# Stick-breaking attention on one Trainium2 core: the first logits ten gate steps earlier, the softplus issued in written order, splits one step behind the sum

## The chip, the cores and the metric

The kernel runs on one core of a Trainium2 chip. The metric is the device time of one execution in microseconds (us). The kernel before takes 1889.11 us, the median of three runs.

The engines are named as in the profile: PE is the matmul engine (PEld its weight loads), DVE the vector engine, ACT the scalar engine, POOL GpSimd, SP the queue that issues the transfers.

## The reference

A decoder trunk of two layers on 512 tokens of width 2048, in float32. The first layer attends to the top keys picked by an indexer, the second is stick-breaking attention over shared keys and values. The change lies in the second:

```python
def mixer_b(x, w_in, w_o, k, v):
    q, gate = jnp.split(x @ w_in, [WIDTH_B], axis=-1)
    ...
        z = jnp.einsum('bqngd,bsnd->bngqs', qg, k).astype(jnp.float32) * (HEAD_DIM ** -0.5)
        strict = key_pos[None, :] < t[:, None]
        log_om = jnp.where(strict, -jax.nn.softplus(z), 0.0)
        suffix = lax.cumsum(log_om, axis=log_om.ndim - 1, reverse=True) - log_om
        a = jnp.where(strict, jnp.exp(jax.nn.log_sigmoid(z) + suffix), 0.0)
        o = jnp.einsum('bngqs,bsnd->bqngd', a.astype(v.dtype), v)
    ...
    return (o * jax.nn.silu(gate)) @ w_o
```

There are 16 query heads in 4 groups; each group shares one head of keys and values. Then come a layer norm and a gated embedding.

## The kernel before

**Split products.** Every float32 operand is split into a high part (ACT copies it to a reduced format, names ending in `h`) and a low part (DVE subtracts, names ending in `l`); `split` does both. `mm3` multiplies high by high, high by low and low by high: three matmuls of 128x512 into one PSUM bank. A *gate step* below is one `mm3` of the gate projection.

**Streams.** Weights arrive through `next_raw` in three buffers `raw`, issued on SP. `Ahead(items, 2)` splits them two items ahead into `wh` and `wl`, three buffers each. `gate_items` also reads back the second half of the eight activation blocks that the Strassen products had overwritten, from `x2` in DRAM, and queues their splits (`restore`, tiles `xh` and `xl`).

**Order.** PE runs in program order (`manual_schedule`). The other engines are ordered by the tile framework's scheduler, except instructions marked by `keep_in_program_order`, which keep their order among themselves. `Paced` marks whatever is issued while `pinned[0]` is set. `bg` is a queue of small pieces of work; `pumped` issues one of them behind each gate step, through `paced`, which pins it.

**The second layer.** Keys, values and queries are Strassen products (loop at L1088, the last one, n == 4, gives the queries of group 3). `combine` adds up the seven products M, first on ACT and DVE, then by three `onto` pieces. Then (L1101 to L1150) the first keys are split, the four query blocks of group 0 and the four value blocks, one piece behind each of the first nine gate steps; 20 gate steps of group 0 run before the pool of the work tiles `px` opens, in the place of the values' unsplit tile.

**Sticks.** `sticks(g, Q)` goes through ten units, the pairs (query block i, key block kb) with kb from i down to 0: unit 0 is (0,0), unit 1 (1,1), unit 2 (1,0), unit 3 (2,2) and so on. The units 0, 1, 3 and 6 are diagonal. For each unit:

- `logits(u)`: z on PE; softplus as Abs, Exp, Ln on ACT and a sum on DVE; the mask `strict` on POOL (L1157) on diagonal units; the split into `sh`, `sl`.
- `weights(u)`: matmuls of `tri` and `neg` by the split softplus add the suffix sums onto z (L1199); Exp on ACT; mask on diagonal units; split into `ah`, `al`.
- `values(u)`: product with the split values into the bank o.

In round s it runs logits(s), weights(s-1), values(s-2), with a yield behind each, and `interleave` puts gate steps of the same group between the yields: 40 of them over 34 yields in group 0 (20 were done before), 52 over 34 in groups 1 to 3, where 8 run ahead. Group 0 has four more yields ahead of its first weights, and so have the others. Behind each group its banks are gated by Silu, which needs another activation table than Exp and Ln; `preload_act_table_set` puts the log and exp table back at the head of each group.

Of the kernel before, what the change touches and what calls it, by code (L numbers as in the profile page):

```python
# [51 lines left out]
def steps(gen, n):  # L52
    for _ in range(n):
        next(gen, None)
# [23 lines left out]
def trunk_kernel(  # L78
# [50 lines left out]
    def split(hi, lo, src, eng=dve):  # L129
        act.activation(hi, src, AF.Copy)  # L130
        eng.tensor_tensor(lo, src, hi.bitcast(F32), ALU.subtract)
# [171 lines left out]
    bg = deque()  # L303

    def paced(fn, *args):
        pinned[0] = True
        fn(*args)
        pinned[0] = False

    def one():  # L310
        paced(bg.popleft())
# [1 line left out]
    def pumped(gen, every=1):  # L313

        for i, _ in enumerate(gen):
            if bg and i % every == 0:
                one()
            yield

    def drain():  # L320
        while bg:
            one()
# [59 lines left out]
    def quarter(x, i, j0=0, rows=2):  # L382

        j = j0 + rows * (i % 2 == 0)
        t = H * (i in (1, 2))
        return x[:, j : j + rows, t : t + H]

    def combine(wp, M, dst):

        m1, m2, m6, m7, m5, m3, m4 = M  # L390
        u = wp.tile([128, 2, H], F32, name="u", tag="u", bufs=1)[:, : m1.shape[1]]
        c11, c22, c12, c21 = (dst(i) for i in range(4))
        pinned[0] = True
        act.activation(u, m1, AF.Copy)
        act.activation(c21, m7, AF.Copy)
        act.activation(c12, m5, AF.Copy)
        dve.tensor_tensor(c11, m2, u, ALU.add)
        dve.tensor_tensor(u, m6, u, ALU.add)
        pinned[0] = False

        def onto(c):
            dve.tensor_tensor(c, c, u, ALU.add)

        def rest():
            dve.tensor_tensor(c22, c12, c21, ALU.add)
            dve.tensor_tensor(c12, m3, c12, ALU.add)
            dve.tensor_tensor(c21, c21, m4, ALU.subtract)

        paced(rest)
        return [lambda c=c: onto(c) for c in (c12, c21, c22)]  # L410
# [124 lines left out]
    def mm_banks(name):  # L535
        return [bank(j, name) for j in range(4)]
# [531 lines left out]
    finish_layer(0, xT, x2, (pk_, pv_), first_sums, first_blocks)  # L1068


    with ps_:
        sp = ps_.enter_context(tc.tile_pool(name="sp1", bufs=1))
        C3.extend(c3_tiles(sp, range(4, 8)))
        Kf, Vf = shared
        banks = [bank(b, "k") for b in range(4)]
        gemm = gemm_w(kitems, plain, banks, order=PAIRS)
        items = first_chunk(gemm, TF, T1, C3, lambda: strassen_stream([512] * 5, sp))
        for g in range(4):
            act.activation(Kf[:, g], banks[g], AF.Copy)

        def turn_values(t):
            s = slice(t * 128, (t + 1) * 128)
            ps = bank(2, "vt")
            for g in range(4):
                pe.transpose(ps[:, g * 128 : (g + 1) * 128], Vf[:, g, s], ident)
            act.activation(Vf[:, :, s], ps.rearrange("p (g d) -> p g d", g=4), AF.Copy)

        for n, dst in enumerate((Vf, *F)):  # L1088
            M = product_banks(4 - n)
            gemm = pumped(gemm_s(items, C3, M), 8)  # L1090
            if n == 1:
                steps(gemm, 40)
                for t in range(4):
                    steps(gemm, 16)
                    turn_values(t)
            run(gemm)
            drain()
            bg.extend(combine(sp, M, lambda i: quarter(dst, i)))
        drain()

# [5 lines left out]
    def split_keys(g):  # L1106
        K[g] = tuple(pc.tile([128, T], F32R, name=f"k{s}", tag=f"k{s}", bufs=2) for s in "hl")
        split(*K[g], Kf[:, g])

    def split_values(t):  # L1110
        split(*V[t], Vf[:, :, t * 128 : (t + 1) * 128])
# [5 lines left out]
        dve.scalar_tensor_tensor(ql, src, HSCALE, qh.bitcast(F32), ALU.mult, ALU.subtract)  # L1117
        Q[i] = tuple(a.rearrange("p h q -> p (h q)") for a in (qh, ql))

    def restore(raw, k):  # L1120
        split(XH[k][:, H:T], XL[k][:, H:T], raw[:, k % 4])

    def gate_items():
        for k, n in ((0, 6), (4, 2)):
            yield from plain_items([(512, n)])
            raw = next_raw()
            bg.extend(lambda raw=raw, k=k: restore(raw, k) for k in range(k, k + 4))
        yield from plain_items([(512, 8), *[(512, NK)] * 3])

    items = Ahead(gate_items(), 2)  # L1130

    def gate_first(banks):

        for kb in (*range(8, NK), *range(8)):
# [3 lines left out]
                mm3(out, (wh[:, s], wl[:, s]), plain(kb), kb == 8, kb == 7)  # L1138
                yield

    bg.append(lambda: split_keys(0))
    for i in range(4):
        bg.append(lambda i=i: split_scaled(0, i))
        bg.append(lambda i=i: split_values(i))
    banks = mm_banks("g")
    gemm = pumped(gate_first(banks))
    steps(gemm, 20)
    pv_.close()
    px_ = ExitStack()
    px = px_.enter_context(ss(name="px", bufs=1, side="right"))  # L1150

    def work():
        return px.tile([128, 512], F32, name="wk", tag="wk", bufs=4)
# [5 lines left out]
    def sticks(g, Q):  # L1159
        units = [(i, kb) for i in range(4) for kb in range(i, -1, -1)]  # L1160
        later = {}
        running = {}
        state = {}
        out = {}

        def logits(u):
            i, kb = units[u]
            z = spare("z")
            ks = slice(kb * 128, (kb + 1) * 128)
            mm3(z, [k[:, ks] for k in K[g]], Q[i], True, True)  # L1170
            e = work()
            keep = kb == i > 1
            sp = px.tile([128, 512], F32, name="run", tag="run", bufs=2) if keep else work()
            act.activation(e, z, AF.Abs)
            act.activation(e, e, AF.Exp, scale=-1.0)
            act.activation(e, e, AF.Ln, bias=1.0)
            dve.scalar_tensor_tensor(sp, z, 0.0, e, ALU.max, ALU.add)
            if kb == i:
                strict(sp)
            parts = tuple(px.tile([128, 512], F32R, name=f"s{s}", tag=f"s{s}", bufs=4) for s in "hl")  # L1180
            split(*parts, sp)
            state[u] = z, parts
            if keep:
                running[i] = sp
            if kb == i:
                later[u + 1] = parts
            elif kb:
                below = tuple(px.tile([128, 512], F32R, name=f"r{s}", tag=f"s{s}", bufs=4) for s in "hl")
                dve.tensor_tensor(running[i], running[i], sp, ALU.add)
                dve.tensor_copy(below[0], running[i])  # L1190
                dve.tensor_tensor(below[1], running[i], below[0].bitcast(F32), ALU.subtract)
                later[u + 1] = below

        def weights(u):
            i, kb = units[u]
            z, parts = state[u]
            terms = [(neg, p) for p in (later[u] if kb < i else ())] + [(tri, p) for p in parts]
            for n, (m, p) in enumerate(terms, 1):
                pe.matmul(z, m, p, start=False, stop=n == len(terms), skip_group_check=True)  # L1199
            a = work()  # L1200
            act.activation(a, z, AF.Exp)
            if kb == i:
                strict(a)
            parts = tuple(px.tile([128, 512], F32R, name=f"a{s}", tag=f"a{s}", bufs=2) for s in "hl")
            split(*parts, a)
            state[u] = parts

        def values(u):
            i, kb = units[u]
            if kb == i:  # L1210
                out[i] = bank(7, "o")
            mm3(out[i], [v[:, g] for v in V[kb]], state.pop(u), kb == i, kb == 0)
            if kb == 0:
                act.activation(F[g][:, :, i * 128 : (i + 1) * 128], out[i].rearrange("p (h q) -> p h q", h=4), AF.Copy)

        for s in range(12):
            for fn, u in ((logits, s), (weights, s - 1), (values, s - 2)):
                if s == 1 and fn == weights:
                    for _ in range(4):
                        yield  # L1220
                if 0 <= u < 10:
                    fn(u)
                    yield

    for g in range(4):
        tc.keep_in_program_order(act.preload_act_table_set("natural_log_exp_and_others"))
        if g:
            banks = mm_banks("g")
            gemm = pumped(gemm_w(items, plain, banks))
        if g < 3:  # L1230
            bg.append(lambda g=g: split_keys(g + 1))
        interleave(sticks(g, Q), 30 + 4, gemm, 52 if g else 40, lead=8 * (g > 0))
        if g < 3:
            for i in range(4):
                split_scaled(g + 1, i)
        for h in range(4):
            sg = work()
            act.activation(sg, banks[h], AF.Silu)
            dve.tensor_tensor(F[g][:, h], F[g][:, h], sg, ALU.mult)
# [52 lines left out]
```

## Time and profile before

| | |
|---|---|
| median of 3 runs | 1889.11 us (1888.52 to 1889.22) |
| the profiled execution | 1889.62 us |
| its span | 1887.9 us |
| PE busy | 1874.2 us (99%) |
| DVE, ACT, POOL busy | 1220.4, 928.5, 28.4 us |
| chain that ended last, by engine | PE 96%, DVE 2%, ACT 1%, DMA 1% |

The span runs from the first to the last instruction of the profiled execution. A timeline row gives start, duration, engine, line, operation, the tiles out<-in and their shapes; the bracket at its end is the idle time of the engine ahead of it and what ended it. The stick-breaking stage lies between about 1243 and 1513 us.

### The profile page before, as it was taken

Reading aid. Unit: us, or ns where it says so; the run is one execution under the profiler, and the core shown is the slowest. Engines: PE = TensorE matmul, PEld = TensorE weight load, DVE = VectorE, ACT = ScalarE, POOL = GpSimd, SP = SyncE. Lnnn points to the kernel's source line nnn. Section 1 sums busy time; section 2 is a strip of 40 time slices with the busy share of each in tenths; the row PEclk is TensorE's granted clock in tenths of the full one; section 3 lists DMA queues with packets and bytes.
Section 4 is the critical chain, followed back from the end, with each engine's and each line's share of the span. In section 5 each row is a group of like instructions: output and inputs, shape, how many; then the busy total and the mean of one; then the engine's idle time right before and its main releaser. Section 6 shows DMA issues by size and latency. Waiting matters only on the chain.

```text
span 1887.9 us, 25064 instructions
## 1 busy us (share of the span) xinstructions
PE 1874.2 (99%) x9229; PEld 1584.7 (84%) x9229; DVE 1220.4 (65%) x2385; ACT 928.5 (49%) x1692; POOL 28.4 (2%) x49
## 2 busy tenths in 40 slices
PE   9999999999999999999999999999999999999998
PEld 7898888888888888888888999987888888888887
DVE  5668879966556454675368788876655545567534
ACT  4446323355554432474245444468877743347422
POOL 0000000000000000000000000000100000000000
PEclk9999999999999999999999999999999999999999
DMA  5432333312222532333343333331122153242333
GB/s 185 137 114 65 101 90 100 101 56 68 67 68 60 165 110 78 124 100 106 117 134 113 106 97 111 101 112 57 56 68 68 57 189 98 75 129 89 123 101 112
DMA packets 110587, 189.22 MB, mean 100 GB/s; under 512 B 8240, under 2 KB 28208, under 8 KB 110464
## 3 DMA queue, kind: packets, MB, share of 16 engines
q1 hardware_dynamic: 110320, 187.33, 32.3%
q8 instruction: 72, 1.18, 0.3%
q14 instruction: 51, 0.42, 0.1%
q0 software_dynamic: 144, 0.30, 0.1%
HBM read 179.21 MB, written 8.39 MB: 99 GB/s over the span
## 4 chain that ended last, share of the span: by engine, by line
PE 96%; DVE 2%; ACT 1%; DMA 1%; issue 1%; SPq 0%; DVEq 0%; ACTq 0%
PE g L134 12%; PE g L135 12%; PE g L136 12%; PE o L135 7%; PE o L136 7%; PE o L134 7%; PE m L134 3%; PE m L135 3%; PE m L136 3%; PE q L135 3%; PE q L136 3%; PE q L134 3%; PE z L1199 2%; PE k L136 2%; PE k L135 2%; PE k L134 2%
## 5 line engine op out<-in xcount | busy, mean ns | idle before, releaser
L111 ACT ACTIVATE wh<-raw 128x512 fp32r<-128x512 f32 (+3 forms) x684 | 396.4, 581 | 674.9 <-PE g L135 239.4
L111 DVE TENSOR_TENSOR wl<-raw,wh 128x512 fp32r<-128x512 f32 (+3 forms) x684 | 430.0, 630 | 430.9 <-ACT wh L111 411.6
L134 PE MATMUL g<-xh,wh 128*128 128x512 f32 x1024 | 404.3, 395 | 0.2
L135 PE MATMUL g<-xl,wh 128*128 128x512 f32 x1024 | 400.6, 391 | 0.6 <-DVE xl L111 0.6
L136 PE MATMUL g<-xh,wl 128*128 128x512 f32 x1024 | 399.9, 391 | 0.0
L134 PEld LDWEIGHTS g<-xh,wh 128*128 128x128 f32 x1024 | 192.6, 188 | 41.0 <-ACT sg L111 1.4
L136 PEld LDWEIGHTS g<-xh,wl 128*128 128x128 f32 x1024 | 192.2, 188 | 41.2
L135 PEld LDWEIGHTS g<-xl,wh 128*128 128x128 f32 x1024 | 192.5, 188 | 38.7 <-DVE xl L111 1.4
L136 PE MATMUL o<-xh,wl 128*128 128x512 f32 x512 | 199.3, 389 | 0.0
L135 PE MATMUL o<-xl,wh 128*128 128x512 f32 x512 | 199.2, 389 | 0.0
L134 PE MATMUL o<-xh,wh 128*128 128x512 f32 x512 | 199.2, 389 | 0.0
L136 PEld LDWEIGHTS o<-xh,wl 128*128 128x128 f32 x512 | 96.1, 188 | 20.3 <-DVE wl L111 0.4
L135 PEld LDWEIGHTS o<-xl,wh 128*128 128x128 f32 x512 | 96.1, 188 | 20.0
L134 PEld LDWEIGHTS o<-xh,wh 128*128 128x128 f32 x512 | 96.1, 188 | 19.9
L134 PE MATMUL q<-xh,wh 128*128 128x512 f32 x256 | 99.6, 389 | 0.0
L135 PE MATMUL q<-xl,wh 128*128 128x512 f32 x256 | 99.6, 389 | 0.0
L136 PE MATMUL q<-xh,wl 128*128 128x512 f32 x256 | 99.6, 389 | 0.0
L111 ACT ACTIVATE sh<-st 128x512 fp32r<-128x512 f32 x80 | 49.0, 628 | 79.7 <-PE m L135 42.5
L111 DVE TENSOR_TENSOR sl<-st,sh 128x512 fp32r<-128x512 f32 x80 | 54.5, 691 | 37.2 <-ACT sh L111 37.2
L111 DVE TENSOR_TENSOR xl<-f,xh 128x512 fp32r<-128x512 f32 x80 | 54.3, 687 | 11.4 <-ACT f L111 11.0
L111 ACT ACTIVATE wk<-z 128x512 f32<-128x512 f32 x80 | 47.3, 591 | 25.2 <-PE z L136 17.2
L134 PEld LDWEIGHTS q<-xh,wh 128*128 128x128 f32 x256 | 48.1, 188 | 10.1
(290 smaller groups left out, 3366.8 us busy)
## 6 DMA issues: line engine op xcount, KB each, us to landing
raw<-w_in_a SPq DMA_DIRECT2D x95, 512.0 KB, 3.7
raw<-w_in_b SPq DMA_DIRECT2D x64, 512.0 KB, 3.8
raw<-w_ple_gate SPq DMA_DIRECT2D x52, 512.0 KB, 3.8
raw<-w_o_a SPq DMA_DIRECT2D x24, 512.0 KB, 3.8
raw<-w_o_b SPq DMA_DIRECT2D x24, 512.0 KB, 3.7
raw<-w_kv_b SPq DMA_DIRECT2D x16, 512.0 KB, 3.8
raw<-w_ple_gate SPq DMA_DIRECT2D x24, 256.0 KB, 2.9
f<-xT SPq DMA_DIRECT2D x4, 1024.0 KB, 6.2
```

The source lines that it names most:

```text
L111: ins = method(*args, **kw)
L134: pe.matmul(out, a[0], b[0], start=start, stop=False)
L135: pe.matmul(out, a[0], b[1], start=False, stop=False)
L136: pe.matmul(out, a[1], b[0], start=False, stop=stop)
L1199: pe.matmul(z, m, p, start=False, stop=n == len(terms), skip_group_check=True)
```

## The change

It moves the first group's start and pins it. The gate items of the second layer are made, and two of them split, ahead of the last combine. Behind the combine come, in written order (`pinned[0]` stays set, and `paced` now restores what it found): the load of the log and exp table, the first keys, two query blocks, ten gate steps, unit 0's logits, four gate steps with value and query splits behind them, unit 0's split and unit 1's logits, five gate steps with the other value splits and four restores, unit 1's split and unit 0's weights. From there on `interleave` spreads the other 45 gate steps of group 0 over the 27 yields that are left.

In all groups the split of a softplus (`stick_parts`) and of a weight (`weight_split`) is issued one yield behind its sum. The pool `px` lies on the other side and opens ahead of the values' release; only the tiles `ah`, `al` lie in the released place (`pal`). The query splits of the next group are pinned.

```diff
     def paced(fn, *args):
-        pinned[0] = True
+        was, pinned[0] = pinned[0], True
         fn(*args)
-        pinned[0] = False
+        pinned[0] = was
...
             drain()
+            if n == 4:
+                items = Ahead(gate_items(), 2).prime()
             bg.extend(combine(sp, M, lambda i: quarter(dst, i)))
...
-    bg.append(lambda: split_keys(0))
-    for i in range(4):
-        bg.append(lambda i=i: split_scaled(0, i))
-        bg.append(lambda i=i: split_values(i))
-    banks = mm_banks("g")
-    gemm = pumped(gate_first(banks))
-    steps(gemm, 20)
-    pv_.close()
+    px = pc_.enter_context(ss(name="px", bufs=1))
     px_ = ExitStack()
-    px = px_.enter_context(ss(name="px", bufs=1, side="right"))
+
+    def log_exp():
+        tc.keep_in_program_order(act.preload_act_table_set("natural_log_exp_and_others"))
...
             dve.scalar_tensor_tensor(sp, z, 0.0, e, ALU.max, ALU.add)
             if kb == i:
                 strict(sp)
+            if keep:
+                running[i] = sp
+            state[u] = z, sp
+            return lambda: stick_parts(u)
+
+        def stick_parts(u):
+            i, kb = units[u]
+            z, sp = state[u]
             parts = tuple(px.tile([128, 512], F32R, name=f"s{s}", tag=f"s{s}", bufs=4) for s in "hl")
             split(*parts, sp)
...
             if kb == i:
                 strict(a)
-            parts = tuple(px.tile([128, 512], F32R, name=f"a{s}", tag=f"a{s}", bufs=2) for s in "hl")
+            return lambda: weight_split(u, a)
+
+        def weight_split(u, a):
+            parts = tuple(pa_late[0].tile([128, 512], F32R, name=f"a{s}", tag=f"a{s}", bufs=2) for s in "hl")
             split(*parts, a)
...
             for fn, u in ((logits, s), (weights, s - 1), (values, s - 2)):
-                if s == 1 and fn == weights:
-                    for _ in range(4):
-                        yield
                 if 0 <= u < 10:
-                    fn(u)
+                    rest = fn(u)
+                    if s == 1 and fn == logits and g:
+                        for _ in range(4):
+                            yield
                     yield
+                    if rest:
+                        rest()
+
+    log_exp()
+    pinned[0] = True
+    split_keys(0)
+    for i in range(2):
+        split_scaled(0, i)
+    banks = mm_banks("g")
+    gemm = pumped(gate_first(banks))
+    steps(gemm, 10)
+    first = sticks(0, Q)
+    steps(first, 1)
+    for i in range(4):
+        bg.append(lambda i=i: split_values(i))
+        if i < 2:
+            bg.append(lambda i=i: split_scaled(0, i + 2))
+    steps(gemm, 4)
+    steps(first, 1)
+    steps(gemm, 5)
+    drain()
+    pv_.close()
+    pa_late = [px_.enter_context(ss(name="pal", bufs=1, side="right"))]
+    steps(first, 1)
+    pinned[0] = False
 
     for g in range(4):
-        tc.keep_in_program_order(act.preload_act_table_set("natural_log_exp_and_others"))
         if g:
+            log_exp()
...
-        interleave(sticks(g, Q), 30 + 4, gemm, 52 if g else 40, lead=8 * (g > 0))
+        if g:
+            interleave(sticks(g, Q), 30 + 4, gemm, 52, lead=8)
+        else:
+            interleave(first, 30 - 3, gemm, 64 - 19)
         if g < 3:
             for i in range(4):
-                split_scaled(g + 1, i)
+                paced(split_scaled, g + 1, i)
```

More of the change, by code (lines that the diff above doesn't have):

```diff
@@ L1068, in trunk_kernel, with restore, gate_items @@
     finish_layer(0, xT, x2, (pk_, pv_), first_sums, first_blocks)
+    def restore(raw, k):
+        split(XH[k][:, H:T], XL[k][:, H:T], raw[:, k % 4])
+    def gate_items():
+        for k, n in ((0, 6), (4, 2)):
+            yield from plain_items([(512, n)])
+            raw = next_raw()
+            bg.extend(lambda raw=raw, k=k: restore(raw, k) for k in range(k, k + 4))
+        yield from plain_items([(512, 8), *[(512, NK)] * 3])
     with ps_:
@@ L1118, in split_scaled @@
         Q[i] = tuple(a.rearrange("p h q -> p (h q)") for a in (qh, ql))
[L1120 to L1130, printed above, removed]
     def gate_first(banks):
@@ L1182, in logits @@
             state[u] = z, parts
-            if keep:
-                running[i] = sp
             if kb == i:
```

## The prediction

> **What bounds the kernel now.** I read the page's first two parts, then the busy time of each engine by stretches around the start of the stick-breaking stage, then the timeline of each engine there.
>
> ```profile
> span 1887.9 us, 25064 instructions
> ...
> PE 1874.2 (99%) x9229; PEld 1584.7 (84%) x9229; DVE 1220.4 (65%) x2385; ACT 928.5 (49%) x1692; POOL 28.4 (2%) x49
> ...
> 1250.00:1260.00 10.00, 10.00 (x46) 8.29 (x45) 9.00 (x18) 9.56 (x19) 0.00 (x0) 1.00 0.43 125
> 1260.00:1265.00 5.00, 3.80 (x17) 2.66 (x15) 3.23 (x7) 4.38 (x10) 0.64 (x1) 1.00 0.45 155
> 1265.00:1275.00 10.00, 9.46 (x39) 7.02 (x39) 6.55 (x11) 9.14 (x19) 1.91 (x3) 1.00 0.33 105
> 1275.00:1285.00 10.00, 9.26 (x40) 6.98 (x39) 7.49 (x12) 8.26 (x17) 1.66 (x2) 1.00 0.17 54
> 1285.00:1310.00 25.00, 25.00 (x109) 19.96 (x108) 17.52 (x28) 20.58 (x37) 1.27 (x2) 1.00 0.14 43
> ...
> 1320.00:1376.00 56.00, 56.00 (x244) 45.42 (x243) 35.79 (x56) 44.04 (x80) 5.85 (x8) 1.00 0.20 64
> ```
>
> In the stretches the columns are width, then busy time (and count) of PE, PEld, DVE, ACT, POOL, then the granted clock and the DMA share. TensorE is busy 1874.2 of 1887.9 us, so all its idle time is 13.7 us. The change removes and adds no matmul; it only reorders. It can win only idle time of TensorE. Inside the part that it moves, that idle time lies between 1260 and 1285 us, where the first group's attention starts; from 1285 on, and in the whole second group (1320 to 1376), PE is full. ACT is the crowded engine here: 9.56 us of 10 before the gap.
>
> The matmuls around the gap, with the idle time before each and what ended it:
>
> ```profile
> 1243.50 0.40 PE L134 MATMUL g<-xh,wh 128*128 128x512 f32 x1
> ...
> 1257.12 0.39 PE L134 MATMUL z<-qh,kh 128*128 128x512 f32 x1
> ...
> 1263.02 0.39 PE L136 MATMUL g<-xh,wl 128*128 128x512 f32 x1
> 1264.61 0.49 PE L1199 MATMUL z<-sh,tri 128*128 128x512 f32 x1 [1.20 <-ACT sh L111]
> 1265.34 0.49 PE L1199 MATMUL z<-sl,tri 128*128 128x512 f32 x1 [0.23 <-DVE sl L111]
> 1265.67 0.39 PE L134 MATMUL g<-xh,wh 128*128 128x512 f32 x1
> ...
> 1267.76 0.39 PE L1199 MATMUL z<-sh,tri 128*128 128x512 f32 x1
> 1268.43 0.49 PE L1199 MATMUL z<-sl,tri 128*128 128x512 f32 x1 [0.28 <-DVE sl L111]
> 1268.76 0.39 PE L134 MATMUL g<-xh,wh 128*128 128x512 f32 x1
> ...
> 1269.46 0.40 PE L134 MATMUL o<-ah,vh 128*128 128x512 f32 x1
> 1269.89 0.50 PE L135 MATMUL o<-al,vh 128*128 128x512 f32 x1
> 1270.23 0.40 PE L136 MATMUL o<-ah,vl 128*128 128x512 f32 x1
> ...
> 1277.42 0.39 PE L136 MATMUL g<-xh,wl 128*128 128x512 f32 x1
> 1278.33 0.50 PE L1199 MATMUL z<-sh,tri 128*128 128x512 f32 x1 [0.51 <-ACT sh L111]
> 1279.05 0.50 PE L1199 MATMUL z<-sl,tri 128*128 128x512 f32 x1 [0.23 <-DVE sl L111]
> 1279.39 0.39 PE L134 MATMUL g<-xh,wh 128*128 128x512 f32 x1
> ```
>
> From 1243.50 to 1257.12 stand 20 gate steps of three matmuls, 13.62 / 60 = 0.227 us from start to start. I call the lost time of a matmul its distance from the one before, less 0.23. For unit 0 (the first weights step) that is 1.36 + 0.50, and 0.10 on the matmul behind it: 1.96. For unit 1, 0.44 + 0.10 = 0.54. For the first values step 0.20 + 0.11 = 0.31. For unit 3 (the diagonal block of the third query row, 1278.33) 0.68 + 0.49 + 0.11 = 1.28. Together **4.09 us**: what the change could win at most here, 0.22% of the time.
>
> Why unit 0 waits is in the ACT, DVE and POOL timelines:
>
> ```profile
> 1249.19 0.62 ACT L111 ACTIVATE vh<-E 128x512 fp32r<-128x512 f32 x1
> 1249.71 0.61 ACT L111 ACTIVATE qh<-f 128x512 fp32r<-128x512 f32 x1
> ...
> 1254.92 1.32 ACT L111 ACTIVATE xh<-raw 128x256 fp32r<-128x256 f32 x4
> 1256.26 1.28 ACT L111 ACT_TABLE_LOAD   x1
> ...
> 1258.61 0.58 ACT L111 ACTIVATE wk<-z 128x512 f32<-128x512 f32 x1
> 1259.61 1.29 ACT L111 ACTIVATE wk<-wk 128x512 f32<-128x512 f32 x2
> ...
> 1261.97 0.63 ACT L111 ACTIVATE wh<-raw 128x512 fp32r<-128x512 f32 x1 [0.58 <-DMA raw<-w_in_b]
> 1262.50 1.01 ACT L111 ACTIVATE xh<-raw 128x256 fp32r<-128x256 f32 x3
> ...
> 1263.94 0.61 ACT L111 ACTIVATE sh<-wk 128x512 fp32r<-128x512 f32 x1
> ...
> 1242.33 0.68 DVE L111 TENSOR_TENSOR f<-m,u 128x512 f32<-128x512 f32 x1
> 1243.12 0.69 DVE L111 TENSOR_TENSOR u<-m,u 128x512 f32<-128x512 f32 x1
> ...
> 1244.34 0.68 DVE L111 TENSOR_TENSOR wl<-raw,wh 128x512 fp32r<-128x512 f32 x1
> ...
> 1246.14 1.89 DVE L111 TENSOR_TENSOR f<-f,u 128x512 f32<-128x512 f32 x3
> ...
> 1256.02 1.43 DVE L111 TENSOR_TENSOR xl<-raw,xh 128x256 fp32r<-128x256 f32 x4
> ...
> 1264.59 0.69 DVE L111 TENSOR_TENSOR sl<-wk,sh 128x512 fp32r<-128x512 f32 x1 [0.26 <-ACT sh L111]
> ...
> 1261.76 0.64 POOL L1157 TENSOR_SCALAR_AFFINE_SELECT wk<-wk 128x512 f32<-128x512 f32 x1 [1071.36 <-DVE wk L111]
> ```
>
> Unit 0's masked softplus was done on POOL at 1261.76 + 0.64 = 1262.40, but ACT sat on a gate weight still in transfer and on three restores, and made `sh` only at 1263.94. Prices from these rows: a queued ACT copy 0.52 us (1249.19 to 1249.71), a chained pair 1.29 (0.64 each), the z read 0.58, a restore 1.32 / 4 = 0.33 on ACT and 1.43 / 4 = 0.36 on DVE, a DVE operation 0.69, and (1.89 - 0.69) / 2 = 0.60 from start to start in a queue; POOL's mask 0.64.
>
> **The change part by part.** *First logits at gate step 10 instead of 20.* No instruction is added. z0 leaves PE ten steps, 10 x 0.68 = 6.8 us, earlier, and its weights step comes after gate step 19 instead of 27. The first keys, two query blocks and the first gate splits must now be ready sooner, and all are pinned in program order. On DVE that order puts the third gate weight's `wl` behind the last combine (in the trace it slips in at 1244.34). The combine has eight operations from 1242.33: the second at 1243.12, then 0.60 apart, so keys and two queries start at 1247.3, 1247.9 and 1248.5, and `wl` at 1249.1, ending at 1249.8. PE wants it for the third matmul of gate step 8, at 1243.50 + 26 x 0.227 = 1249.4: a new wait of **0.44 us**. It shifts all that follows alike, so z0's last matmul starts at 1251.2 and ends at 1251.6.
>
> *The table load* (1.28 us) goes from 1256.26 to right behind the combine's ACT copies, about 1243.7. ACT then makes the keys, two queries and a gate split by 1247.2, ahead of DVE; its cover is that z0 comes only at 1251.2, and without it the load would sit in the softplus chain at 1.28. I take nothing.
>
> *Softplus beside the conversions of values, in pinned order.* From z0's end ACT has: absolute value, exponential, logarithm (0.05 latency + 0.60 + 0.64, next start 0.52 on); value split, query split, gate split, value split, query split, unit 0's `sh` (6 x 0.52 = 3.12); unit 1's softplus (0.60 + 0.64 + 0.52); two value splits and a gate split (1.56); four restores (1.32); then unit 1's `sh`. Unit 0's `sh` starts 1.81 + 2.60 = 4.41 us after z0's end, at 1256.0, and DVE, which adds unit 0's sum at 1253.5 and has five splits queued behind it, gives `sl` at 1253.5 + 6 x 0.60 + 0.69 = 1257.8. PE reaches unit 0's weights step 30 matmuls after z0's last one (four gate steps, z1, five gate steps), at 1251.2 + 31 x 0.227 = 1258.2. So unit 0's loss of **1.96 us goes**, with half a microsecond to spare.
>
> Unit 1 is next late. Its `sh` starts 1.81 + 3.12 + 1.76 + 1.56 + 1.32 = 9.57 us after z0's end and lands at 9.57 + 0.68 = 10.25, at 1261.8. PE gets there after only 39 matmul distances, 39 x 0.227 = 8.85 from the start of z0's last matmul, 1260.0. That is a wait of **1.80 us**; then `sl` follows on DVE behind the same restores at 1262.2 and lands at 1262.94, against 1262.06 wanted: **0.88** more. POOL is no part of it: z1's mask ends near 1259.9, before ACT is free. Behind the waiting matmul stands all of PE's order, gate steps too, although these have their data. The pinned stretch therefore loses 0.44 + 1.80 + 0.88 + about 0.2 of slow restarts = 3.3 us, where the same steps (units 0 and 1, the first values) now lose 1.96 + 0.54 + 0.31 = 2.8.
>
> *Gate steps saved for later.* Group 0 has 64 - 19 = 45 gate steps behind the remaining 27 stick steps, 1.67 each, instead of 40 / 34 = 1.18. Groups 1 to 3 have 52 / 34 = 1.53 and the second loses nothing (56.00 of 56.00). So unit 3's **1.28 us should go**. Written-out order with the durations above would still leave up to 1.5 us of small waits behind unit 1 (a split held behind one operation); the scheduler, free again there, has avoided such waits in the second group, so I take 0.2, nearest to the row of 1320 to 1376.
>
> *Parts one step behind the sum.* Same count of instructions in all groups, with the split of a softplus or weight emitted one yield later. In groups 1 to 3 the cover is the 1.53 gate steps on each side; bounds are 0 (no idle time is there to win) and one ACT slot for each of the 12 diagonal units, 12 x 0.52 = 6.2 us. I take 0, by the same row.
>
> *Transfers.* SP issues the same weight loads and the same two reads of x2 in the same order; priming two gate items ahead of the combine asks for splits that the scheduler already hoists. The restores now run from 1259.8 instead of 1254.92, which frees that buffer for the next weight about 5 us later; that weight is wanted eight gate steps after its split is queued, so nothing. Pinning the next group's query splits moves 0.52 us apiece on ACT in mid-group: nothing.
>
> Sum: -1.96 - 0.54 - 0.31 - 1.28 + 3.3 + 0.2 = **-0.6 us**. The profiled execution took 1889.62 us, 1.7 over its span and 0.5 over the median of three, 1889.11. I give it against the median: **1888.5 us**. About 0.2% (3.8 us) is what a measurement of this kernel can tell from no change, so this is no change.
>
> **The rivals.** *All waits vanish.* If the scheduler or the real order lets unit 1's `sh` past the restores and the value splits, each of the six waits goes: 1889.1 - 4.1 = 1885.0 us. For it: value splits have no urgent reader, and unit 1's softplus is on POOL by 1259.9. Against it: restores and splits are all pinned ahead of `sh`, and their sum on ACT is fixed.
>
> *Late splits turn into waits in groups 1 to 3* (slower). A diagonal unit's split goes through POOL and back to ACT; emitted one step later, it can land behind a gate split, 0.52 us. At 12 places that is 6.2 us: 1888.5 + 6.2 = 1894.7. It decides if the units there have less than 0.2 us of slack on the mean. For it: ACT is 44.04 / 56 = 79% busy there, and unit 3 in group 0 shows such a wait today. Against it: not one of those waits shows in 1320 to 1376, and a list order that follows readiness does not care which of two came first in the text.
>
> *Unit 1's wait is longer.* Three more operations ahead of it (the next keys, a gate split, a query) make 3 x 0.52 = 1.6 us: 1890.1 us. The stretch from 1260 to 1265, with 1.20 us of idle time, keeps a granted clock of 1.00. The Trainium skill, TensorE: Matmul & The Clock Gate, "What's actually happening", says that TensorE's clock halves after an idle window of about 3.4 us; no wait in these rows is that long. By that page a wait of 3.4 us would cost up to another 1.7 us of half-speed time (an estimate from the page), 1891.8.
>
> *The change does not do what it says*: the scheduler restores the present order, 1889.1.
>
> **How the numbers follow.** Forecast 0.57, all within 0.2%; late splits 0.18, slower; all waits vanish 0.12, faster; the longer wait 0.07 and no effect 0.06, both within. The late splits are counted slower at their full size. The tails of the forecast's unknowns (a re-made schedule of everything behind 1240 us) move 0.04, half to each side. So faster 0.14, same 0.66, slower 0.20. The forecast's own range is 1886.6 to 1890.6; reaching to the first rival and to half of the second gives 1885.0 to 1891.8.
>
> **What would show it.** z0 near 1251 us and unit 0's weights near 1258 with no idle time before it; a wait of about 1.8 us before the third weights matmul pair (unit 1) ended by ACT `sh`, then 0.9 by DVE `sl`; 0.4 us at gate step 8 ended by DVE `wl`; no wait at unit 3; 56.00 of 56 in the later groups. Idle time spread over groups 1 to 3 would prove the late splits; a stretch from 1243 to 1285 without any would prove the first rival. A difference that lies outside 1240 to 1510 us would make the whole reading wrong.

## The result and the profile after

The changed kernel takes **1897.02 us** (median of 5; before 1889.11): 1.0042 times as long, 95% interval 1.0031 to 1.0052. The forecast was 1888.5 us, between 1885.0 and 1891.8. It is 7.9 us slower, where I had expected no change. The profiled execution took 1896.03 us, the fastest of the five; its span is 6.4 us longer than the one before.

The page's first lines and the busy time by stretches of the changed kernel, with the columns of the prediction's first fence:

```profile
span 1894.3 us, 25045 instructions
...
PE 1874.8 (99%) x9229; PEld 1587.6 (84%) x9229; DVE 1220.5 (64%) x2385; ACT 929.7 (49%) x1692; POOL 30.3 (2%) x49
...
1240.00:1250.00 10.00, 9.11 (x51) 7.38 (x49) 8.04 (x13) 6.49 (x11) 0.00 (x0) 1.00 0.18 53
...
1260.00:1265.00 5.00, 1.70 (x6) 0.91 (x5) 4.49 (x9) 4.40 (x11) 2.43 (x2) 0.85 0.13 17
1265.00:1275.00 10.00, 10.00 (x34) 7.93 (x34) 5.20 (x8) 7.87 (x16) 1.21 (x2) 0.73 0.26 97
...
1310.00:1320.00 10.00, 8.45 (x36) 6.34 (x35) 5.81 (x11) 8.83 (x16) 0.00 (x0) 1.00 0.18 54
1320.00:1376.00 56.00, 56.00 (x247) 46.11 (x247) 34.63 (x54) 43.48 (x77) 5.85 (x8) 1.00 0.22 66
...
1383.00:1442.00 59.00, 57.35 (x250) 46.95 (x251) 37.23 (x58) 46.91 (x82) 5.85 (x8) 1.00 0.23 70
1442.00:1452.00 10.00, 8.23 (x36) 6.46 (x36) 4.67 (x8) 7.14 (x12) 0.00 (x0) 1.00 0.19 57
```

The reader sees four things. PE has a hole between 1260 and 1265 us, far larger than the old one. Behind it PE counts as busy, but makes 34 matmuls in 10 us instead of 39, at a granted clock of 0.73. Three new holes lie at 1310 to 1320, 1383 to 1442 and 1442 to 1452, where the groups change. And in the full stretch 1320 to 1376 there are 247 matmuls instead of 244. In the kernel before, the first and the last of these three stretches read:

```profile
1310.00:1320.00 10.00, 9.89 (x44) 7.84 (x43) 5.48 (x9) 7.71 (x12) 0.00 (x0) 1.00 0.25 68
...
1442.00:1452.00 10.00, 10.00 (x46) 8.19 (x45) 6.06 (x10) 8.57 (x13) 0.00 (x0) 1.00 0.33 93
```

The matmuls of the changed kernel that had to wait, or that came slowly:

```profile
1249.24 0.50 PE L134 MATMUL g<-xh,wh 128*128 128x512 f32 x1 [0.86 <-ACT wh L111]
...
1250.21 0.50 PE L136 MATMUL g<-xh,wl 128*128 128x512 f32 x1 [0.24 <-DVE wl L111]
...
1262.86 0.50 PE L1200 MATMUL z<-sh,tri 128*128 128x512 f32 x1 [2.11 <-ACT sh L111]
1264.55 0.80 PE L1200 MATMUL z<-sl,tri 128*128 128x512 f32 x1 [1.19 <-DVE sl L111]
1265.14 0.63 PE L134 MATMUL g<-xh,wh 128*128 128x512 f32 x1
1265.57 0.63 PE L135 MATMUL g<-xl,wh 128*128 128x512 f32 x1
...
1318.26 0.50 PE L134 MATMUL g<-xh,wh 128*128 128x512 f32 x1 [0.99 <-ACT wk L111]
...
1319.78 0.50 PE L134 MATMUL g<-xh,wh 128*128 128x512 f32 x1 [0.56 <-ACT wk L111]
...
1384.51 0.50 PE L134 MATMUL g<-xh,wh 128*128 128x512 f32 x1 [1.77 <-ACT wk L111]
...
1451.75 0.50 PE L134 MATMUL g<-xh,wh 128*128 128x512 f32 x1 [1.77 <-ACT wk L111]
```

Counted as in the prediction (distance from the matmul before, less 0.23), the losses are:

| place | before, us | after, us |
|---|---|---|
| gate step 8 | 0 | 1.64 |
| unit 0 | 1.96 | 0 |
| unit 1 | 0.54 | 3.73 |
| matmuls at 0.43 instead of 0.227, 1265.1 to 1270.5 | 0 | 2.77 |
| first values | 0.31 | 0 |
| unit 3 | 1.28 | 0 |
| heads of groups 1, 2, 3 | 0.37 + 0.34 + 0 | 2.08 + 2.44 + 2.04 |

Between 1240 and 1530 us all such losses come to 5.2 us before and 14.7 after, 9.5 more. The shorter distance gives back 2.4 us: from the first gate step to the last values step lie 1117 distances in both kernels, and without the losses they come to 257.26 us before and 254.85 after. Together 7.1 us, and by that much the stretch grew (1243.50 to 1505.92 before, 1242.75 to 1512.30 after). The profiled execution of the changed kernel came to the stage 0.74 us earlier, which leaves the 6.4 us of the spans; the other edits' executions, too, reach it between 1242.6 and 1243.6 us.

### The profile page after: what moved, and what is told of

Read it like the earlier page. It is cut to its first block, busy times and chain, and to the rows that moved or that the text cites. A ratio compares the mean times of both kernels' runs of the same rounds, so it can differ in the third digit from the quotient of the medians.

```text
span 1894.3 us, 25045 instructions
## 1 busy us (share of the span) xinstructions
PE 1874.8 (99%) x9229; PEld 1587.6 (84%) x9229; DVE 1220.5 (64%) x2385; ACT 929.7 (49%) x1692; POOL 30.3 (2%) x49
## 4 chain that ended last, share of the span: by engine, by line
PE 95%; DVE 2%; ACT 2%; issue 1%; DMA 0%; SPq 0%; DVEq 0%; ACTq 0%
PE g L134 12%; PE g L135 12%; PE g L136 12%; PE o L136 7%; PE o L134 7%; PE o L135 7%; PE m L134 3%; PE m L135 3%; PE m L136 3%; PE q L134 3%; PE q L135 3%; PE q L136 3%; PE k L135 2%; PE k L136 2%; PE k L134 2%; PE z L1200 2%
## 5 line engine op out<-in xcount | busy, mean ns | idle before, releaser
L136 PEld LDWEIGHTS q<-xh,wl 128*128 128x128 f32 x256 | 48.1, 188 | 10.0
```

What stands on the lines that cost most here:

```text
L136: pe.matmul(out, a[1], b[0], start=False, stop=stop)
```

## The experiments

Theory 1: the query splits, now pinned, hold up the Silu that frees the gate banks at each group's head. Theory 2: unit 1's split is late in ACT's and DVE's queues, and the long wait lowers TensorE's clock. Theory 3: where the work tiles lie sets the distance of the matmuls. The rivals stand with each run. Names with a are edits of the changed kernel, with b of the kernel before; each was compared with the kernel before in the same set (1888.8 to 1889.1 us).

**a_queries_free.**

```diff
-                paced(split_scaled, g + 1, i)
+                split_scaled(g + 1, i)
```

> The changed kernel with one word undone: the next group's query splits are no longer pinned. Theory 1 (the pinned splits, four copies of 0.52 us, are held behind the group's last units and stand ahead of the Silu that frees the gate banks): the waits at the heads of groups 1, 2 and 3, 2.08 + 2.44 + 2.04 us against 0.37 + 0.34 + 0 before, go back; about 5.8 us less, 1891.2 us. Rival (the heads wait because splits one step behind make each group's last units end late): the waits stay, 1897 us. The wait before unit 1 and the slow matmuls behind it stay in both.

Measured 1891.19 us, 1.0011 of the kernel before (1.0002 to 1.0020). The heads lose 0, 0.37 and 0 us. Theory 1 holds; the rival does not. The hole before unit 1 stays (4.25 us), and in the profiled execution the slow matmuls behind it too.

**b_queries_pinned**, the same word alone in the kernel before.

```diff
-                split_scaled(g + 1, i)
+                paced(split_scaled, g + 1, i)
```

> The kernel before with the next group's query splits pinned and nothing else. Theory 1: waits of about 2 us at the heads of groups 1, 2 and 3, some 5.8 us more, 1895 us. Rival (splits one step behind): 1889 us.

Measured 1893.38 us, 1.0024 (1.0014 to 1.0033), 4.3 us more. Its PE timeline at the first and the last of the three heads:

```profile
1313.23 0.50 PE L134 MATMUL g<-xh,wh 128*128 128x512 f32 x1 [1.75 <-ACT wk L111]
...
1448.93 0.50 PE L134 MATMUL g<-xh,wh 128*128 128x512 f32 x1 [1.75 <-ACT wk L111]
```

The heads lose 2.44 + 2.44 + 2.02 = 6.9 us, 6.2 more than before. I had missed what the move gives back in mid-group, where the splits no longer take ACT's time: unit 3 loses 0.33 instead of 1.28, the first values nothing. 6.2 - 0.95 - 0.31 = 4.9, near the 4.3 measured. So the pinning alone, without any other part, makes the waits at the heads.

How it does so shows in ACT's timeline of the changed kernel at the head of group 1:

```profile
1312.78 1.28 ACT L111 ACT_TABLE_LOAD   x1
1314.07 1.09 ACT L111 ACTIVATE wk<-g 128x512 f32<-128x512 f32 x2
1315.04 0.60 ACT L111 ACTIVATE f<-o 128x512 f32<-128x512 f32 x1
1315.52 2.20 ACT L111 ACTIVATE qh<-f 128x512 fp32r<-128x512 f32 x4
1317.60 0.60 ACT L111 ACTIVATE wk<-g 128x512 f32<-128x512 f32 x1
...
1319.12 0.61 ACT L111 ACTIVATE wk<-g 128x512 f32<-128x512 f32 x1
```

`wk<-g` is the Silu of a gate bank. Two of the four are made, then come the group's last output copy `f<-o` and four query splits, 2.1 us, and only then the third and fourth Silu, for which PE waits at 1318.26 and 1319.78. (At the two later heads all four splits stand ahead of the table load and of every Silu, and PE waits once, 1.77 us.) In the kernel before, the splits for group 1 started at 1259.1, 1267.9, 1282.9 and 1301.4 us, and three Silu followed the table load without a break:

```profile
1301.39 0.62 ACT L111 ACTIVATE qh<-f 128x512 fp32r<-128x512 f32 x1
...
1312.29 1.58 ACT L111 ACTIVATE wk<-g 128x512 f32<-128x512 f32 x3
```

**a_restores_late.**

```diff
+    held = []
...
-            bg.extend(lambda raw=raw, k=k: restore(raw, k) for k in range(k, k + 4))
+            (held if k == 0 else bg).extend(lambda raw=raw, k=k: restore(raw, k) for k in range(k, k + 4))
...
     steps(first, 1)
+    bg.extend(held)
     pinned[0] = False
```

> The changed kernel with the first four restores queued behind unit 0's weights instead of ahead of unit 1's split. Theory 2 (unit 1's split is late in ACT's and DVE's queues, and the long wait lowers TensorE's granted clock): the split comes 1.3 us earlier on ACT and 1.4 us or more on DVE, so the loss before unit 1 falls from 3.73 to 1.5 us or less, the granted clock stays at 1.00 and the 2.8 us of slow matmuls behind it go too; about 5 us less, 1892 us. Rival (the slow matmuls come from something else, such as SBUF traffic of POOL and DVE): only some 2.2 us less, 1894.8 us, and the clock below 1 stays. Rival (the splits are late for another reason): 1897 us.

Measured 1895.78 us, 1.0037 (1.0024 to 1.0049), only 1.2 us less than the changed kernel. In its timeline of PE, and its stretch from 1260 to 1265:

```profile
1262.92 0.49 PE L1202 MATMUL z<-sh,tri 128*128 128x512 f32 x1 [1.63 <-ACT sh L111]
1264.87 0.50 PE L1202 MATMUL z<-sl,tri 128*128 128x512 f32 x1 [1.45 <-DVE sl L111]
...
1277.07 0.50 PE L1202 MATMUL z<-sh,tri 128*128 128x512 f32 x1 [1.19 <-ACT sh L111]
...
1260.00:1265.00 5.00, 1.93 (x8) 1.07 (x7) 4.81 (x8) 4.96 (x12) 1.81 (x2) 1.00 0.22 59
```

The first half of the expectation failed. Two restores and the next gate split still ran ahead of unit 1's split, which gained little (3.50 us lost instead of 3.73). And unit 3 now lost 1.95 us; the restores that did move run ahead of its splits, but PE also reaches it earlier without the slow matmuls, and the two were not separated. In this execution the clock stayed at 1.00 and no matmul was slow: the 2.77 us went.

That is no proof that a shorter wait saved the clock, for the wait is almost as long. When the clock fell can be read from the trace. In the changed kernel it changes at 7.43, 1263.53, 1270.36 and 1891.59 us, which lie 368, 2 and 182 times 3.413 us apart; the changes in the other runs keep to the same step. The last step before the fall and the 6.83 us of half clock behind it, and then the two steps of a_restores_late over which its wait is spread:

```profile
1260.12:1263.53 3.41, 1.13 (x4) 0.37 (x2) 3.41 (x8) 3.41 (x9) 0.85 (x2) 1.00 0.01 2
1263.53:1270.36 6.83, 5.81 (x14) 4.56 (x15) 4.43 (x7) 4.77 (x9) 2.28 (x2) 0.50 0.47 154
```
```profile
1259.55:1262.96 3.41, 1.78 (x9) 1.15 (x8) 3.39 (x5) 3.40 (x8) 0.96 (x1) 1.00 0.30 106
1262.96:1266.38 3.42, 1.97 (x8) 1.41 (x9) 3.18 (x7) 3.34 (x7) 0.85 (x1) 1.00 0.49 152
```

PE was busy for 1.13 of 3.41 us before the fall. In a_queries_free it was 1.14, and the clock fell at 1263.54, when PE had been idle for 2.27 us and was still waiting. In a_restores_late the border between two steps lies within the wait, PE is busy for 1.78 and 1.97 us of them, and the clock holds. So what counts is how much of one such step the wait fills, and where the border falls was luck. It seems to differ between executions: one of the five of a_restores_late has a mean clock of 0.998, like the changed kernel's 0.997 to 0.998, and seven of the eleven of a_queries_free have 0.999. The Trainium skill, TensorE: Matmul & The Clock Gate, "What's actually happening", puts this window at about 3.4 us and has the clock fall after an idle one; the step agrees, but here the clock fell after a window in which PE was busy for a third of the time.

**a_nine**, a_queries_free with four more gate steps ahead of unit 0's weights.

```diff
-    steps(gemm, 5)
+    steps(gemm, 9)
...
-            interleave(first, 30 - 3, gemm, 64 - 19)
+            interleave(first, 30 - 3, gemm, 64 - 23)
```

> The changed kernel with the query splits free (a_queries_free, 1891.2 us) and nine gate steps instead of five between unit 1's logits and unit 0's weights. Theory 2 (unit 1's split comes a fixed time after z0, so PE waits for what gate work lies between): PE comes 4 x 0.68 = 2.7 us later, the loss before unit 1 falls from 4.25 us to about 1.5, the clock stays at 1.00, and 2.3 us of slow matmuls go: 1891.2 - 2.7 - 2.3 = about 1886 us. Rival (other pieces slip ahead of the split and use up the time): the wait stays above 3 us and the time above 1889 us.

Measured 1887.29 us, 0.9993 (0.9984 to 1.0001), 3.9 less than a_queries_free. The clock stays at 1.00, and here the wait is shorter by more than half. Before unit 1 only the DVE half is left:

```profile
1265.74 0.50 PE L1200 MATMUL z<-sl,tri 128*128 128x512 f32 x1 [1.18 <-DVE sl L111]
```

That is 1.67 us lost instead of 4.25: the theory's 2.7 us earlier, nearly. About 1.3 us of new small waits at the values and 0.6 at unit 3 took much of the rest of the expected 5.

**b_split_late**, the splits one yield behind their sums, alone in the kernel before.

```diff
+            state[u] = z, sp
+            return lambda: stick_parts(u)
+
+        def stick_parts(u):
...
+            return lambda: weight_split(u, a)
+
+        def weight_split(u, a):
...
-                    fn(u)
+                    rest = fn(u)
...
+                    if rest:
+                        rest()
```

> The kernel before with the splits of softplus and weights issued one yield behind their sums, and nothing else. My forecast's step (the free scheduler sees to it): within 1 us of 1889.1 us. Rival (late splits turn into waits on diagonal units): up to 6 us more, 1895 us.

Measured 1888.43 us, 0.9997 (0.9988 to 1.0006). No new wait appears in groups 1 to 3. This part of the change costs nothing that shows here, and my slower rival was wrong.

**b_px_left**, the work tiles' pool on the other side, with the same order of instructions on every engine.

```diff
-    px = px_.enter_context(ss(name="px", bufs=1, side="right"))
+    px = pc_.enter_context(ss(name="px", bufs=1))
```

> The kernel before with the pool of the stick-breaking work tiles on the left side of SBUF, as in the changed kernel, in the same order of instructions. Theory 3 (where these tiles lie sets the distance of matmuls in this stage: 244 in 56 us before, 247 after): the distance falls from about 0.231 to 0.228 us or less between 1265 and 1507 us, some 3 us less, 1886 us. Rival (the distance depends on the order, such as the splits one step behind): 1889 us and 0.231.

Measured **1885.72 us**, 0.9984 (0.9975 to 0.9992), 3.4 us less. PE, ACT, DVE and POOL run the same instructions in the same order as before, and the waits are the same (5.1 us in all against 5.2); the matmuls come closer together. The next five runs ask what it is in the place, with a small tile put between (here 8 floats, 32 bytes, on the left):

```diff
+    pad = pc_.enter_context(ss(name="pad", bufs=1)).tile([128, 8], F32, name="pad"); pool.memset(pad, 0.0); px = pc_.enter_context(ss(name="px", bufs=1))
```

> The kernel before with a tile of 32 bytes per partition put next to the work tiles' pool on the right side, so that the same tiles lie 32 bytes lower; one 32-byte fill on POOL is added. The two places tried so far differ by 38.09 - 36 = 2.09 KB, which is 33.5 times 64 bytes. Theory 4 (matmuls that read these tiles go slower when the tiles do not start on a multiple of 64 bytes): the distance falls from 0.231 to 0.227 us and the time to about 1886 us. Rival (the region or the neighbour of the tiles counts, not 32 bytes): 1889 us and 0.231.

> The kernel before with the work tiles on the left, as in b_px_left, but 32 bytes higher. Theory 4 (multiples of 64 bytes): the gain of b_px_left is lost, distance 0.231 and 1889 us. Rival (the left side is what helps): 1886 us and 0.227.

> As b_left_pad32 (1888.6 us), with 64 bytes. If multiples of 64 bytes are enough: 0.227 and 1886 us. Theory 5 (128 or more): 0.231 and 1889 us, as b_right_pad32 suggests, which lay at the same remainder.

> As b_left_pad64, with 128 bytes. If multiples of 128 bytes are enough: 0.227 and 1886 us. If the multiple has to be larger, or any shift of the tiles hurts: 0.231 and 1889 us.

> As b_right_pad32 (1889.1 us), with 96 bytes: the tiles then lie 2.09 KB - 96 bytes = 2048 bytes above their place in b_px_left. Theory 5 (a multiple of 128 bytes or more is what counts; 32 bytes lower left them at 64 past a multiple of 128): distance 0.227, 1886 us. Rival (the region counts): 0.231, 1889 us.

The stretch 1320 to 1376 of b_px_left, b_left_pad32, b_left_pad64, b_left_pad128, b_right_pad32 and b_right_pad96:

```profile
1320.00:1376.00 56.00, 56.00 (x247) 46.12 (x247) 35.73 (x56) 44.59 (x81) 5.88 (x8) 1.00 0.19 57
```
```profile
1320.00:1376.00 56.00, 56.00 (x244) 45.53 (x243) 35.46 (x55) 43.95 (x80) 5.88 (x8) 1.00 0.19 60
```
```profile
1320.00:1376.00 56.00, 56.00 (x244) 45.43 (x243) 35.87 (x56) 44.16 (x80) 5.86 (x8) 1.00 0.21 64
```
```profile
1320.00:1376.00 56.00, 56.00 (x245) 45.62 (x245) 35.52 (x56) 44.11 (x79) 5.86 (x8) 1.00 0.19 57
```
```profile
1320.00:1376.00 56.00, 56.00 (x244) 45.42 (x243) 35.89 (x56) 44.21 (x80) 5.87 (x8) 1.00 0.21 65
```
```profile
1320.00:1376.00 56.00, 56.00 (x248) 46.13 (x247) 36.05 (x56) 44.60 (x80) 5.88 (x8) 1.00 0.19 57
```

The kernel before has its tiles 2144 bytes above their place in b_px_left; that comes from the places of the pools (38.09 and 36 KB), which no trace shows.

| tiles, from their place in b_px_left | us | ratio to before (95%) |
|---|---|---|
| b_px_left, 0 | 1885.72 | 0.9984 (0.9975 to 0.9992) |
| b_left_pad32, +32 bytes | 1888.61 | 0.9999 (0.9990 to 1.0008) |
| b_left_pad64, +64 | 1889.27 | 1.0000 (0.9991 to 1.0010) |
| b_left_pad128, +128 | 1887.77 | 0.9994 (0.9985 to 1.0003) |
| kernel before, +2144 | 1889.0 | 1 |
| b_right_pad32, +2112 | 1889.11 | 1.0003 (0.9994 to 1.0012) |
| b_right_pad96, +2048 | 1885.95 | 0.9983 (0.9974 to 0.9992) |

Theory 4 (64 bytes) fell: 32 bytes on the right changed nothing, 64 on the left cost all of the gain. Theory 5 stands as far as it goes: 2048 bytes away the gain is back in full, on the right side too, so not the side counts but the offset. At +128 part of the gain seems to be back (245 matmuls, 1.2 us less), but the interval reaches beyond 1. If a multiple is what counts, the one that suffices lies above 128 and at or below 2048 bytes; that was not tried.

**a_best**, a_nine with the split weights' tiles on the left and one gate step ahead of the keys.

```diff
+    banks = mm_banks("g")
+    gemm = pumped(gate_first(banks))
+    steps(gemm, 1)
     split_keys(0)
     for i in range(2):
         split_scaled(0, i)
-    banks = mm_banks("g")
-    gemm = pumped(gate_first(banks))
-    steps(gemm, 10)
+    steps(gemm, 9)
...
-    pa_late = [px_.enter_context(ss(name="pal", bufs=1, side="right"))]
+    pa_late = [pc_.enter_context(ss(name="pal", bufs=1))]
```

> a_nine (1887.3 us) with two more edits: the tiles of the split weights lie on the left too, and the first gate step is issued ahead of the keys' split, so that the third gate weight is split before the keys. Theory: the loss of 1.64 us at gate step 8 goes (the weight no longer waits behind the keys, which wait for the last combine), and the distance falls from 0.228 to 0.227 us, 0.5 us more: about 1885.2 us, the level of b_px_left (1885.7) or below it. Rival (the keys are then later and z0 waits for them instead): 1886.8 us.

Measured **1884.85 us**, 0.9977 (0.9968 to 0.9986): 4.1 us less than the kernel before and 12 less than the changed one. PE is busy 10.00 of 10 us from 1240 to 1250, and 248 matmuls lie between 1320 and 1376. The two edits were not tried one by one.

## Why the prediction was wrong

**The step that failed first: "Pinning the next group's query splits moves 0.52 us apiece on ACT in mid-group: nothing."** I took the mark to keep marked instructions in order among themselves, as the section on the kernel says. That is too weak. By the rows, a marked instruction is also held behind the one issued just before it on its engine, marked or not: ACT's timeline above has all four query splits behind the group's last `f<-o`, which is not marked, where the kernel before spread them over the group. What hid them, ACT's idle time in mid-group, was gone, and I had not asked what they cost without that cover: 5.85 us, against nothing forecast. a_queries_free takes it away, and b_queries_pinned makes 6.2 us of it from nothing else.

**Unit 1's wait was the right mechanism and too small.** I had 1.80 + 0.88 = 2.68 us; it was 2.28 + 1.45 = 3.73. ACT and DVE in the changed kernel:

```profile
1261.68 0.61 ACT L111 ACTIVATE wh<-raw 128x512 fp32r<-128x512 f32 x1
1262.20 0.61 ACT L111 ACTIVATE sh<-wk 128x512 fp32r<-128x512 f32 x1
...
1255.28 1.12 DVE L111 SCALAR_TENSOR_TENSOR ql<-f,qh 128x512 fp32r<-128x512 f32 x1
...
1259.62 1.72 DVE L111 TENSOR_TENSOR vl<-E,vh 128x512 fp32r<-128x512 f32 x2
...
1263.21 0.68 DVE L111 TENSOR_TENSOR wl<-raw,wh 128x512 fp32r<-128x512 f32 x1
1263.81 0.68 DVE L111 TENSOR_TENSOR sl<-wk,sh 128x512 fp32r<-128x512 f32 x1
...
1259.84 0.96 POOL L1152 TENSOR_SCALAR_AFFINE_SELECT wk<-wk 128x512 f32<-128x512 f32 x1 [3.98 <-DVE wk L111]
```

The next gate weight, not pinned, slipped in ahead of the split, 0.52 us on ACT and 0.60 on DVE; that is about the whole of the 1.05 us that my sum lacked. Beside the masks of POOL, DVE's operations took longer (1.12 instead of 0.69), and the mask itself 0.96 instead of 0.64. My sum used durations from rows in which POOL and DVE did not run side by side; how much of the wait this makes was not separated.

**The price of a long wait.** I had the clock as a rival at 0.07, for a wait of 3.4 us. It fell after 2.27 us without a matmul in a_queries_free, and it cost 2.77 us in the changed kernel, where I had up to 1.7. No run shows that 1.7: the clock was at 0.50 for two steps of 3.41 us, not one. What I had missed is that a wait of this length can fill most of one step or be cut in two by a border, so that 2.68 us may already have been within reach of it. The upper end of my range, 1891.8, is that estimate's; half of the late splits would have given 1888.5 + 3.1 = 1891.6.

**Gate step 8** lost 1.64 us instead of 0.44. I had the keys' split start when ACT was free; it waited for DVE's last combine, in both kernels:

```profile
1242.97 1.28 ACT L111 ACT_TABLE_LOAD   x1
1246.99 0.63 ACT L111 ACTIVATE kh<-E 128x512 fp32r<-128x512 f32 x1 [2.73 <-DVE f L111]
1247.53 1.14 ACT L111 ACTIVATE qh<-f 128x512 fp32r<-128x512 f32 x2
1248.57 1.65 ACT L111 ACTIVATE wh<-raw 128x512 fp32r<-128x512 f32 x3
...
1244.99 1.89 DVE L111 TENSOR_TENSOR f<-f,u 128x512 f32<-128x512 f32 x3
```

The idle time of 2.73 us behind the table load ends with the last `f<-f,u`, at 1246.9. The kernel before has the same kind of wait (1.28 us; its keys' split started at 1248.13, its last combine ended at 1248.03), but there the gate split was not queued behind the keys. The reason is probably that the keys' tiles lie where the combine's had been; that was not tried. a_best, with the gate split ahead, loses nothing there.

**What held.** Unit 0's wait went, unit 3's and the values' too. Unit 0's went narrowly: its low part was ready at 1258.81 for a matmul at 1258.95, and in a_queries_free the same matmul waited and unit 0 lost 0.61 us. The splits one step behind cost nothing (b_split_late). None of the large waits ended with a transfer. What I did not have at all is the gain of 2.4 us from the place of the tiles; without it the change would have lost some 10 us.

Added up, the stage was forecast to be 0.6 us shorter and was 7.1 longer. Of these 7.7 us the heads make 5.85, the slow matmuls 2.77, gate step 8 1.20 and unit 1 1.05; the place of the tiles takes 2.4 off, and the rest are small waits that I had forecast, or that were there before, and that did not come.

## What to carry to other kernels

Ask of every mark of order what exactly it ties to what, and where in the queue the marked work ends up; work that hid in idle time costs its full length when it is moved to where all engines meet. Where a sum over a queue comes near a limit with a step in its price, as TensorE's clock here, which fell after 3.41 us with PE busy for 1.13, the chance has to follow the sum's error. Moving tiles can change the time by itself: compare the distance of equal instructions in a full stretch before reading a difference as order.

## What was not expected of the hardware

The distance of matmuls in a full stretch depends on the byte offset of the tiles that are read or written beside them. With the order of all engines unchanged, 2144 bytes make 244 instead of 247 matmuls in 56 us, and 3.4 us in the kernel. The matmuls that read these tiles are among the slower ones; in the changed kernel, where only the split weights lay at the other offset, the mean distance was 0.2267 us between the two matmuls of `neg` and the split softplus, and 0.236 between the first two of a values step. But they are not the only ones. Between the second and the third matmul of a gate step, which read none of the moved tiles, the mean distance from 1320 to 1376 us is 0.2307 in the kernel before and 0.2270 in b_px_left, so something other than PE's own reads of these tiles must have a part in it. Shifts of 32 and 64 bytes spoil the good place, a shift of 2048 keeps it. Which engine's access is the slow one stays open.

The clock changes only at steps of 3.413 us. It fell after steps in which PE was busy for 1.13 and 1.14 us, and held through steps with 1.66 us at the heads of b_queries_pinned; so the limit, if it is one of PE's busy time, lies between. It did not come back after the first step behind the fall, in which PE was busy for 2.40 us, but after the second, a full one: 5.1 us of back-to-back matmuls (1265.14 to 1270.26) ran at half clock.
